# An interleave of two arrays in fp32: loads and stores spread over three DMA queues

## The chip, the cores and the metric

The kernel runs on one core of a Trainium2 chip. Times are device microseconds of one execution, and the figure compared is the median over several runs. The profile comes from one further execution, recorded by the hardware profiler; its own time and its span are given beside the median below.

Engines appear by short names: DVE is VectorE, ACT is ScalarE, POOL is GpSimd, SP is SyncE. A "q" behind the name (ACTq) means the engine's instruction queue, which issues DMAs. A DMA issued by any of them is carried out by the core's 16 DMA engines.

## The reference

Two arrays of 32 x 256 x 1024 fp32 (33.55 MB each) are interleaved element by element along the last axis:

```python
def reference(x, y):
    batch, seq, dim = x.shape               # 32, 256, 1024
    result = np.zeros((batch, seq, dim * 2), dtype=np.float32)
    result[..., 0::2] = x
    result[..., 1::2] = y
    return result
```

Nothing is computed; 67.1 MB are read and 67.1 MB written. Because the interleave pairs element k of x with element k of y, all three arrays can be treated as flat.

## The kernel before

**Tiles.** Each input is cut into 8 tiles of 128 partitions x 8192 fp32 (`WL`). A partition's row is 32 KB and contiguous in memory, so a tile is one contiguous 4.19 MB block and a load is 128 rows of 32 KB. Tile i of x and of y (`xtile`, `ytile`) are loaded at lines 56 and 57, both by SP. Each pool has two buffers, so the load of tile i+2 must wait until tile i has been copied.

**Copies and stores.** Every tile is worked off in two halves of 4096 columns (`WS`). For each half, line 70 copies x's half into the even columns of `otile`, and line 71 copies y's half into the odd columns, both on DVE. `otile` is 128 x 8192 fp32, so the store of one half (line 72, issued by ACT) is again 128 rows of 32 KB, 4.19 MB. `otile` has two buffers too: the copies of half n need the store of half n-2 to have landed. There are 16 loads, 32 copies and 16 stores.

**A first write.** Before the loop a small tile of zeros (16 x 128) is set by DVE (line 45) and written to the start of 16 output rows by ACT (line 47). The real stores write over it later.

**Order.** Every engine works through its own instructions in order, and semaphores order them among each other. SP's queue holds x0, y0, x1, y1 and so on; a y load is issued after the x load of its tile. ACT's queue holds the zero write and the stores. POOL has nothing in the loop.

**The opening.** After the program has been compiled, lines 86 to 104 take the first DMA that SP issues (x0, which waits for nothing) out of the body, and put it into the opening block ahead of SP's `Drain`, which belongs to the barrier of all engines at the start. So x0 is issued before that barrier, at 0.00 us of the span.

Of the kernel before, what the change touches and what calls it, by code (L numbers as in the profile page):

```python
# [2 lines left out]

# [4 lines left out]


@with_exitstack
def _interleave(
    ctx: ExitStack,
    tc: tile.TileContext,
    x: bass.AP,
    y: bass.AP,
    out: bass.AP,
):
    nc = tc.nc
    P = 128  # L20

    total = 1
    for s in x.shape:
        total *= s

    WL = 8192
    WS = 4096

    xf = x.rearrange("b s d -> (b s d)")
    yf = y.rearrange("b s d -> (b s d)")  # L30
    of = out.rearrange("b s d -> (b s d)")

    fp32 = mybir.dt.float32

    xpool = ctx.enter_context(tc.tile_pool(name="xp", bufs=2))
    ypool = ctx.enter_context(tc.tile_pool(name="yp", bufs=2))
    opool = ctx.enter_context(tc.tile_pool(name="op", bufs=2))

    lwidths = [WL] * (total // P // WL)
    assert sum(lwidths) == total // P  # L40


    wpool = ctx.enter_context(tc.tile_pool(name="wp", bufs=1))
    zero = wpool.tile([16, 128], fp32, name="zero")
    nc.vector.memset(zero, 0.0)  # L45
    first = dataclasses.replace(of, offset=0, ap=[[2 * WL, 16], [1, 128]])
    nc.scalar.dma_start(out=first, in_=zero)

    start = 0
    for lw in lwidths:  # L50
        xtile = xpool.tile([P, WL], fp32, name="xtile")[:, :lw]
        ytile = ypool.tile([P, WL], fp32, name="ytile")[:, :lw]

        xs = dataclasses.replace(xf, offset=start, ap=[[lw, P], [1, lw]])
        ys = dataclasses.replace(yf, offset=start, ap=[[lw, P], [1, lw]])
        nc.sync.dma_start(out=xtile, in_=xs)
        nc.sync.dma_start(out=ytile, in_=ys)

        soff = 0
        while soff < lw:  # L60
            width = min(WS, lw - soff)
            otile = opool.tile([P, 2 * WS], fp32, name="otile")[:, : 2 * width]
            os_ = dataclasses.replace(
                of,
                offset=2 * start + 2 * soff,
                ap=[[2 * lw, P], [1, 2 * width]],
            )
            xsub = xtile[:, soff : soff + width]
            ysub = ytile[:, soff : soff + width]
            nc.vector.tensor_copy(out=otile[:, 0::2], in_=xsub)  # L70
            nc.vector.tensor_copy(out=otile[:, 1::2], in_=ysub)  # L71
            nc.scalar.dma_start(out=os_, in_=otile)
            soff += width

        start += P * lw
    assert start == total


def kernel(tc, x, y, out):
    nc = tc.nc  # L80
    _interleave(tc, x, y, out)
    tc.close()
    tc.compile()  # L83


    blocks = nc.main_func.blocks
    opening = blocks[0].instructions
    at, moved = next(
        (b, i)
        for b in blocks[1:]  # L90
        for i in b.instructions
        if i.engine == mybir.EngineType.SP and i.opcode == "DMACopy"
    )
    assert not moved.sync_info.on_wait
    body = at.instructions
    body.remove(moved)
    gate = next(
        n
        for n, i in enumerate(opening)
        if i.engine == mybir.EngineType.SP and i.opcode == "Drain"  # L100
    )
    opening.insert(gate, moved)
    at.instructions = body
    blocks[0].instructions = opening


# [1 line left out]
_INS = ['x', 'y']  # L108
_OUTS = [((32, 256, 2048), 'float32')]


# [23 lines left out]
```

## Time and profile before

| | us |
|---|---|
| median of 4 runs | 315.93 (315.63 to 316.23) |
| the profiled execution's own time | 316.82 |
| its span (first to last instruction) | 315.0 |
| DVE busy | 72.8 |
| copies of line 70: 16, mean | 2.295 |
| copies of line 71: 16, mean | 2.292 |
| DVE idle before line 70, waiting for a store | 180.1 |
| DVE idle before line 71, waiting for y | 34.1 |
| x load, issue to landing (median) | 42.9 |
| y load, issue to landing (median) | 60.0 |
| store, issue to landing (median) | 29.9 |

The profile's page divides the span into 40 slices and gives for each the busy share of DVE and of the DMA engines in tenths, and the GB/s moved. "DMA out_dram<-otile" as the releaser of an idle stretch means that the engine waited for a store to land, which includes the time that the store stood in line. The mean over the span is 426 GB/s.

### The profile page before, as it was taken

How to read it: one execution, taken by the hardware profiler on the slowest of the kernel's cores; microseconds unless marked ns; L12 is line 12 of the kernel's file. 1: busy time of each engine (PE TensorE's matmuls, PEld its weight loads, DVE VectorE, ACT ScalarE, POOL GpSimd, SP SyncE). 2: the span in 40 equal slices, each digit the busy share in tenths (PEclk: the TensorE clock that was granted, in tenths of full speed). 3: DMA queues.
4: the chain of work that ended last, by engine and by line, in shares of the span. 5: the costliest groups of instructions: out<-in, count | busy, mean ns of one | idle time of the engine just before them, and what ended most of it. 6: DMA issues, size and time to landing. Idle time of an engine off the chain costs nothing.

```text
span 315.0 us, 152 instructions
## 1 busy us (share of the span) xinstructions
DVE 72.8 (23%) x33; POOL 0.2 (0%) x4
## 2 busy tenths in 40 slices
DVE  0334002213022220223203241041500405014500
POOL 0000000000000000000000000000000000000000
DMA  9999999999999999999999999999999999999996
GB/s 367 429 441 358 454 412 454 412 454 412 454 412 453 412 454 416 449 420 449 420 445 424 441 424 441 429 437 433 433 433 433 437 429 441 424 441 424 441 424 279
DMA packets 4641, 134.23 MB, mean 426 GB/s; under 512 B 529, under 2 KB 545, under 8 KB 545
## 3 DMA queue, kind: packets, MB, share of 16 engines
q1 hardware_dynamic: 2304, 67.11, 49.9%
q10 hardware_dynamic: 2336, 67.12, 49.3%
q14 instruction: 1, 0.00, 0.0%
HBM read 67.11 MB, written 67.12 MB: 426 GB/s over the span
## 4 chain that ended last, share of the span: by engine, by line
DMA 83%; DVE 11%; DVEq 1%; issue 0%
DMA out_dram<-otile 76%; DMA ytile<-in_y_dram 7%; DVE otile L71 6%; DVE otile L70 5%; DVEq L83 1%; DVEq L70 0%
## 5 line engine op out<-in xcount | busy, mean ns | idle before, releaser
L70 DVE COPY otile<-xtile 128x4096 f32<-128x4096 f32 x16 | 36.6, 2295 | 191.7 <-DMA out_dram<-otile 180.1
L71 DVE COPY otile<-ytile 128x4096 f32<-128x4096 f32 x16 | 36.6, 2292 | 34.1 <-DMA ytile<-in_y_dram 34.1
L45 DVE MEMSET zero<- 16x128 f32 x1 | 0.2, 165 | 0.9 <-PEq L119 0.9
L119 POOL MEMSET const-bfloat16-1.0<- 128x1 bf16 x1 | 0.1, 101 | 0.0
L119 POOL MEMSET const-uint8-127<- 128x1 uint8 x1 | 0.1, 101 | 0.0
L119 POOL MEMSET const-float32-0.0<- 128x1 f32 x1 | 0.1, 98 | 0.2 <-issue 0.2
L119 POOL MEMSET const-float32-1.0<- 128x1 f32 x1 | 0.1, 98 | 0.0
## 6 DMA issues: line engine op xcount, KB each, us to landing
out_dram<-otile ACTq DMA_DIRECT2D x16, 4096.0 KB, 29.9
xtile<-in_x_dram SPq DMA_DIRECT2D x8, 4096.0 KB, 42.9
ytile<-in_y_dram SPq DMA_DIRECT2D x8, 4096.0 KB, 60.0
out_dram<-zero ACTq DMA_DIRECT2D x1, 8.0 KB, 6.7
```

Source lines behind the costliest of these rows:

```text
L45: nc.vector.memset(zero, 0.0)
L70: nc.vector.tensor_copy(out=otile[:, 0::2], in_=xsub)
L71: nc.vector.tensor_copy(out=otile[:, 1::2], in_=ysub)
L83: tc.compile()
L119: nc = _bacc.Bacc("TRN2", target_bir_lowering=False, num_devices=1)
```

## The change

The stores and the zero write are issued by POOL (`nc.gpsimd`) instead of ACT, and the y loads by ACT instead of SP. The step that moves a DMA into the opening is run for SP and for ACT: x0 and y0 are then both issued ahead of the opening barrier, each by its own engine. Tiles, buffers and copies are the same.

```diff
-    nc.scalar.dma_start(out=first, in_=zero)
+    nc.gpsimd.dma_start(out=first, in_=zero)
...
         nc.sync.dma_start(out=xtile, in_=xs)
-        nc.sync.dma_start(out=ytile, in_=ys)
+        nc.scalar.dma_start(out=ytile, in_=ys)
...
-            nc.scalar.dma_start(out=os_, in_=otile)
+            nc.gpsimd.dma_start(out=os_, in_=otile)
...
-    opening = blocks[0].instructions
-    at, moved = next(
-        (b, i)
-        for b in blocks[1:]
-        for i in b.instructions
-        if i.engine == mybir.EngineType.SP and i.opcode == "DMACopy"
-    )
...
+    for engine in (mybir.EngineType.SP, mybir.EngineType.Activation):
+        opening = blocks[0].instructions
+        at, moved = next(
+            (b, i)
+            for b in blocks[1:]
+            for i in b.instructions
+            if i.engine == engine and i.opcode == "DMACopy"
+        )
+        assert not moved.sync_info.on_wait
+        body = at.instructions
+        body.remove(moved)
+        gate = next(
+            n
+            for n, i in enumerate(opening)
+            if i.engine == engine and i.opcode == "Drain"
+        )
+        opening.insert(gate, moved)
+        at.instructions = body
+        blocks[0].instructions = opening
```

More of the change, by code (lines that the diff above doesn't have):

```diff
@@ L86 @@
     blocks = nc.main_func.blocks
-    opening = blocks[0].instructions
-    at, moved = next(
-        (b, i)
-        for b in blocks[1:]
-        for i in b.instructions
-        if i.engine == mybir.EngineType.SP and i.opcode == "DMACopy"
-    )
[L94 to L104, printed above, removed]
+    for engine in (mybir.EngineType.SP, mybir.EngineType.Activation):
[17 more added lines that the diff above has]
+        blocks[0].instructions = opening
 _INS = ['x', 'y']
```

## The prediction

> **What bounds the kernel now.** I read the page first: the engines' busy time, the DMA row, the queue table and the chain.
>
> ```profile
> span 315.0 us, 152 instructions
> ...
> DVE 72.8 (23%) x33; POOL 0.2 (0%) x4
> ...
> DMA  9999999999999999999999999999999999999996
> ...
> q1 hardware_dynamic: 2304, 67.11, 49.9%
> q10 hardware_dynamic: 2336, 67.12, 49.3%
> ...
> DMA out_dram<-otile 76%; DMA ytile<-in_y_dram 7%; DVE otile L71 6%; DVE otile L70 5%; DVEq L83 1%; DVEq L70 0%
> ```
>
> VectorE works a quarter of the span. The 16 DMA engines are busy in every slice, and the two queues (q1 the loads, q10 the stores) fill 99.2% of their time. So VectorE's long waits for stores, and the 76% of the chain on `out_dram<-otile`, are waits for a transfer that stands in line behind others. The second view, stretches of the span with the GB/s in each, shows how much is left.
>
> ```profile
> 0.00:1.00 1.00, 0.14 (x1) 0.20 (x4) 1.00 0.00 0
> 1.00:2.00 1.00, 0.03 (x1) 0.00 (x0) 1.00 1.87 524
> 2.00:22.00 20.00, 4.50 (x2) 0.00 (x0) 1.00 0.97 420
> 22.00:34.00 12.00, 4.50 (x2) 0.00 (x0) 1.00 0.99 390
> 34.00:40.00 6.00, 0.00 (x0) 0.00 (x0) 1.00 1.01 437
> 40.00:312.00 272.00, 63.62 (x28) 0.00 (x0) 1.00 1.00 433
> 312.00:315.00 3.00, 0.00 (x0) 0.00 (x0) 1.00 0.08 33
> ```
>
> The last column is GB/s. From 40 to 312 us it is 433. The trace's records of single DMA packets agree: nearly every 32 KB packet took 1213 ns on its engine, load or store, alone or mixed (16 x 32768 B / 1.213 us = 432 GB/s). All bytes at 433 take 134.23 MB / 433 = 310.0 us, which leaves 5.0 of the 315.0:
> - about 1.0 us before the first byte and 0.4 us of ramp (0 to 22 us moved 8.92 MB, worth 20.6 us);
> - 1.2 us in 22 to 34 us, when the first real stores join: 12 x (433-390)/433. Load packets there took up to 2.9 us by the packet records;
> - the rest, some 2.4 us, at the end: engines that finish up to 1.5 us apart, the last landing, the closing barrier.
>
> The third view is the end, as a timeline, and SP's wait in it.
>
> ```profile
> 282.57 2.29 DVE L70 COPY otile<-xtile 128x4096 f32<-128x4096 f32 x1 [14.93 <-DMA out_dram<-otile]
> 288.87 2.30 DVE L71 COPY otile<-ytile 128x4096 f32<-128x4096 f32 x1 [4.00 <-DMA ytile<-in_y_dram]
> 291.20 8.65 ACTq L72 DMA_DIRECT2D out_dram<-otile  x2
> 294.98 2.29 DVE L70 COPY otile<-xtile 128x4096 f32<-128x4096 f32 x1 [3.81 <-DMA out_dram<-otile]
> 297.19 2.29 DVE L71 COPY otile<-ytile 128x4096 f32<-128x4096 f32 x1
> ```
> ```profile
> SPq L83 <- DMA out_dram<-otile: 19.3, 1, 19.3
> ```
>
> Number the stores 0 to 15. Store 13 lands at 294.9 and releases the last two copies; from there SP waits 19.3 us for stores 14 and 15, 8.39 MB, which is 434 GB/s. So the tail has no hole: store 15, issued at 299.5, was in line before store 14 landed at 294.9 + 9.7 = 304.6.
>
> **The change, part by part.** The bytes, their rate and the 16 engines stay. A cost counts only if it empties the engines or makes a packet slower.
>
> *Opening.* x0 is issued at 0.00 as before. y0 moves from 0.78 us on SP to about the same 0.0 on ACT. x0's packets alone kept the engines full to its landing at 12.6, so the earlier issue moves no byte sooner: gain 0, at most the 0.4 us ramp; at worst the two issues (0.37 us each) delay each other by one, 0.37. I take 0. x0 and y0 now share the engines, so x0 lands near 22 us instead of 12.6, and y0 at the 22.3 it had. The first L70 copies lose their head start (12.63): before, two L70 and one L71 were done by 24.65; now two or three copies of 2.2 to 2.3 us stand between 22.3 and store 0, so it goes out at 26.8 to 29 instead of 24.7, and x2 at about 29 instead of 17.15. Cover: x1 and y1, 8.39 MB = 19.4 us, fill the engines to 41.7. Cost 0.
>
> *y loads off SP.* On SP the y load stands behind x's, and its issue waited 13.5 us in all for L71. On ACT it waits for the same L71. Nothing is behind it there but the next y load. Cost 0. With two load rings against one of stores, I expect loads to take up to two thirds of the rate while both are queued, so y lands with x and the 34.1 us that L71 waits for y go to L70's wait for stores. Work is conserved: the stores get everything once the loads are in. The two buffers per pool still hold x(i+2) and y(i+2) back until the second half of tile i is copied.
>
> *17 stores onto POOL.* POOL has nothing to do after 0.43 us but the barriers, so nothing queues behind a store that waits for its L71, except the next store, which needs a later L71. The price is the time from L71's end to the first byte, which no row of before shows for this queue. From below: it equals ACT's issue, 0.34 us, and the 1.0 us that x0 took from issue to first byte, so 0 more. From above, by the tail: store 15 was issued 5.1 us before store 14 landed; less that 1.0 us, about 4 us are spare. A POOL issue up to 4 us longer costs nothing; beyond, each exposed store pays the excess. I take 0.
>
> *The rule that speaks against it.* The row: an L70 or L71 copy takes 2.29 us for 4096 fp32 per partition, 1.79 elements per ns, more than one per cycle at VectorE's 0.96 GHz. The Trainium skill (SBUF — State Buffer, section "SBUF: two separate sides") says of such two-port fp32 copies that GpSimd is locked out of its SBUF port while they run and cannot write descriptors for a DMA of its own queue; the DMA starts only when the copy ends. No row of before shows a DMA on that queue. Charged to every store at one copy, it is 16 x 2.3 = 37 us and 352. But the timeline shows what runs after an L71: VectorE sits idle, 14.9 or 10.6 us in the middle and 3.81 at the end, because the next copy needs the store before. Only store 0 has copies right behind it (2.2 to 4.5 us), under the 19.4 us of x1 and y1. By the rows the rule costs 0, also where it holds. Even a whole copy of delay, 2.3 us, is inside the 4 us.
>
> *First stores.* The 1.2 us of 22 to 34 us come again with the first store of another queue: gone (-1.2) or doubled (+1.2). The nearest row is the same event in before, so 1.2, change 0. The zero write stays as the queue's first use.
>
> *Packets.* If this queue's descriptors are also one per 32 KB row, 0. The packet records give a price for splitting: 27 ns for 512 B and 1213 for 32 KB make 8.2 ns fixed per packet, so n pieces per row add (n-1) x 8.2 ns x 128 store packets per engine = 1.05 us for each further piece. Fixed above by 4 KB pieces: 7 x 1.05 = 7.3 us. The row has only 32 KB packets; I take 0.
>
> *End.* The closing barrier (0.7 us after the last landing) already runs over POOL: 0, at most some tenths.
>
> **Sum.** 315.0 + 0 = 315.0 for the profiled execution's span. Its own time was 316.82, the median of the runs is 315.93; the runs without a profile are what is compared, so the forecast is 315.93 plus what the small unpriced terms, all on POOL's side (issue, completion), leave: 316.0. A measurement of this kernel can tell 0.2%, 0.6 us, from no change.
>
> **Rivals.**
> - *Faster.* The losses at the opening and the first stores shrink: ramp 0.4, first stores 1.2, and the engines' finish 1.5 us apart halves. For: they are the only non-433 stretches, and they lie where the change acts. Against: the same transfers start the same way. All of it is 0.4 + 1.2 + 0.8 = 2.4, half of it 1.2: 314.7.
> - *Slower by the store packets.* Each store row is cut into pieces on the software queue. It decides from two pieces on (1.05 us, above 0.6); at 4 KB pieces 323.2. For: another generator writes the descriptors. Against: no split in any row here.
> - *Slower by POOL's issue.* If descriptors take more than 4 us beyond ACT's issue, the tail opens: with two stores left that see it, 2 us of excess give 2 x 2 = 4 us, 319.9. Against: ACT's issue takes 0.34 us, a tenth of the slack.
> - *The change doesn't do what it says*, all DMAs being served as before: 315.9, inside the forecast.
>
> **How the numbers follow.** Forecast (316.0, own range 315.3 to 316.5): 0.40. Faster rival 0.26. Slower by packets 0.14, by POOL's issue 0.10, by several tenths from worse first stores or uneven engines 0.10. So faster 0.26, same 0.40, slower 0.34. Leaving out about 0.2, mostly the far end of splitting, the range is 314.7 to 320.0.
>
> **What would show it.** DMA 9 in every slice and 433 GB/s in the middle; three queues, with 67 MB stores on POOL's, 2048 store packets of data; L71's wait for y near 0, and L70's wait for stores up by about 30 us; first L70 near 22 us instead of 12.63; SP's last wait about 19.3 us for two stores. It is wrong if store packets are more than 2048, if GB/s in the store-only tail falls under 433, or if store landings at the end are more than 9.7 us apart: that would be POOL's issue.

## The result, and the profile after

The changed kernel has a median of 316.53 us (44 runs, 316.17 to 320.5) against 315.91 us for the kernel before (63 runs, 315.45 to 317.07). The ratio is 1.0045, with a 95% interval of 1.0033 to 1.0057: slower by about 1.4 us in the mean (the ratio compares means) and by 0.6 us in the median. The forecast was no change, 316.0.

The shape of the 44 times matters more than their median. 26 of them lie between 316.17 and 317.00, with a mean of 316.44; the other 18 lie between 317.16 and 320.5, with a mean of 318.88. Before's 63 runs have a mean of 316.01. So the mean moved by 1.43 us: 0.43 because even the usual run is longer, and 18/44 x (318.88 - 316.44) = 1.00 because of the second group. These are two effects, and the experiments look for the cause of each.

The lowest run rose by more than the usual one: 316.17 against 315.45, or 0.72 us. Before's runs spread over 1.6 us, the 26 usual runs over 0.8, so the usual run gets some of the 0.72 back.

The profiled execution took 316.38 us, a usual run. Before's profiled execution took 316.82, which is one of before's longer runs; what the two profiles show of the end must be compared with that in mind. First the page, in the parts that answer to those shown of before.

```profile
span 314.6 us, 150 instructions
...
DVE 72.0 (23%) x33; POOL 10.8 (3%) x21
...
q0 software_dynamic: 2336, 67.12, 49.4%
q1 hardware_dynamic: 1152, 33.55, 24.9%
q10 hardware_dynamic: 1152, 33.55, 24.9%
...
L71 DVE COPY otile<-xtile 128x4096 f32<-128x4096 f32 x16 | 36.7, 2294 | 225.3 <-DMA out_dram<-otile 143.5
L72 DVE COPY otile<-ytile 128x4096 f32<-128x4096 f32 x16 | 36.6, 2288 | 0.0
```

Three queues share the 16 engines. The stores' queue has 2336 packets, exactly what ACT's queue had: the software queue also makes one packet of each 32 KB row. The same two rows of before:

```profile
L70 DVE COPY otile<-xtile 128x4096 f32<-128x4096 f32 x16 | 36.6, 2295 | 191.7 <-DMA out_dram<-otile 180.1
L71 DVE COPY otile<-ytile 128x4096 f32<-128x4096 f32 x16 | 36.6, 2292 | 34.1 <-DMA ytile<-in_y_dram 34.1
```

The copies of y (now line 72) wait for nothing; their 34.1 us have gone into the wait of the x copies (225.3, against 191.7 + 34.1 = 225.8 before). Next the stretches, with GB/s in the last column.

```profile
1.00:2.00 1.00, 0.17 (x1) 0.52 (x1) 1.00 1.46 459
2.00:22.00 20.00, 0.24 (x1) 0.10 (x1) 1.00 0.97 420
22.00:34.00 12.00, 8.67 (x4) 2.54 (x2) 1.00 1.01 404
34.00:40.00 6.00, 0.00 (x0) 0.00 (x0) 1.00 0.99 426
40.00:312.00 272.00, 62.96 (x28) 7.44 (x14) 1.00 1.00 433
```

Little has moved here: the opening at 420; the dip at the first stores, a little later, with 0.1 MB more moved over the two stretches from 22 to 40 us; 433 in the long middle. By the trace's records of single packets the last packet ends at 312.77 us, where before's profile, of a long run, had 313.92, but the span ends only 0.4 us earlier. The time after the last packet is 1.83 us instead of 1.12, that is 0.71 more, and the lowest runs differ by 0.72. That is where the profile differs, and the next view shows why: the closing line's instructions in the queues of POOL and SP (durations in ns, least/median/most, then first and last start in us), first of before, then of after.

```profile
L83 POOLq EVENT_SEMAPHORE  x4: 17/17/17, 314.4 to 314.9; - x4
L83 POOLq DRAIN  x3: 34/41/70, 0.7 to 314.8; - x3
L83 SPq DRAIN  x3: 7/7/7, 314.3 to 314.6; - x3
```
```profile
L84 POOLq EVENT_SEMAPHORE  x4: 17/17/17, 313.9 to 314.5; - x4
L84 POOLq DRAIN  x3: 34/101/15236, 298.6 to 314.3; - x3
L84 SPq DRAIN  x3: 7/7/7, 313.2 to 314.1; - x3
```

SP has seen the last store land at 313.2 and is ready for the barrier. In before, POOL answers 0.1 us later (314.3, 314.4). In after, POOL has its own drain, issued with the last store at 298.6 and 15.24 us long: it ends at 313.85, 0.7 us after SP was ready, and only then does POOL answer (313.9).

### The profile page after: what moved, and what is told of

Same layout as the page of the kernel before. It is cut to its first block, busy times and chain, and to the rows that moved or that the text cites. A ratio compares the mean times of both kernels' runs of the same rounds, so it can differ in the third digit from the quotient of the medians.

```text
span 314.6 us, 150 instructions
## 1 busy us (share of the span) xinstructions
DVE 72.0 (23%) x33; POOL 10.8 (3%) x21
## 3 DMA queue, kind: packets, MB, share of 16 engines
q0 software_dynamic: 2336, 67.12, 49.4%
## 4 chain that ended last, share of the span: by engine, by line
issue 56%; DMA 31%; DVE 6%; POOL 2%; POOLq 0%; DVEq 0%
DMA out_dram<-otile 24%; DMA xtile<-in_x_dram 7%; DVE otile L71 3%; DVE otile L72 3%; POOL out_dram L73 2%; POOLq L84 0%; POOLq L73 0%; DVEq L71 0%
## 5 line engine op out<-in xcount | busy, mean ns | idle before, releaser
L71 DVE COPY otile<-xtile 128x4096 f32<-128x4096 f32 x16 | 36.7, 2294 | 225.3 <-DMA out_dram<-otile 143.5
L73 POOL DMA_DIRECT2D out_dram<-otile x16 | 10.0, 624 | 287.1 <-DVE otile L72 287.1
```

Source lines behind the costliest of these rows:

```text
L73: nc.gpsimd.dma_start(out=os_, in_=otile)
```

## The experiments

A ring is here the DMA queue of one issuing engine. The software queue is POOL's, which the profile calls `software_dynamic`. Three theories were to explain the two effects: POOL's drain (in every run), the software queue as such, or three rings in place of two. The changed kernel again, both loads on SP, y on POOL, and the last store on ACT were timed together on one chip; the others on other chips, all of them beside the kernel before.

**The changed kernel again.** No edit.

> The changed kernel unaltered, to see how its runs spread beside the others on one chip. Three theories of why its median is 0.6 us above before's and why 20 of 44 runs lie between 317 and 320.5: (drain) POOL's closing drain ends 0.7 us after the last store has landed, in every run; (software queue) stores through POOL's queue lose a further 1.5 to 4 us in some runs; (three rings) it is the two load rings beside the store ring, whatever generates the stores, that throw the 16 engines out of step in some runs. All three expect here a lowest run of 316.2 and about half the runs above 317; the median between 316.4 and 317.5. In the profile: last store landing about 0.7 us ahead of POOL's drain's end.

Measured 316.37 to 319.63, median 316.55; 2 of 12 runs above 317.5, fewer than expected. (The expectation says 20 of the first 44 lie above 317; by the list it is 18, and 17 lie above 317.5.) The profile shows the same end: POOL's drain ends 0.7 us after SP is ready. A third time:

> The changed kernel unaltered, on another occasion, since the kernels with the spare loads were not timed beside it: if the runs above 317 belong to the kernel, some 20 to 40% of them here (0 in 12 would have a chance of about 1 in 50 at 28%), lowest 316.2 to 316.4; if they belonged to one chip or one occasion, none.

316.31 to 319.4, 4 of 12 above 317.5, ratio 1.0046 (1.0025 to 1.0067). The longer runs belong to the kernel: 17, 2 and 4, that is 23 of 68 on three occasions. The share varies between them, from 2 of 12 to 17 of 44.

**Stores on POOL, both loads on SP**, run twice. Only x0 is issued in the opening, as in before.

```diff
-        nc.scalar.dma_start(out=ytile, in_=ys)
+        nc.sync.dma_start(out=ytile, in_=ys)
...
-    for engine in (mybir.EngineType.SP, mybir.EngineType.Activation):
+    for engine in (mybir.EngineType.SP,):
```

> Stores and zero write on POOL, both loads back on SP, only x0 in the opening: two rings. Drain: the lowest run stays 0.7 above before's, 316.2. Software queue: the long runs of 317 to 320 stay. Three rings: the long runs go, all runs within 316.2 to 317.1 (before's own spread of 1.6 plus the drain).

> Both loads on SP, stores on POOL, once more, for the count: if a single load ring keeps the engines together, all runs within 316.5 to 317.3 again; if the spread belongs to the software queue, some runs above 317.5.

316.64 to 317.19 (8 runs) and 316.59 to 317.09 (11 runs), ratio 1.0022 (1.0014 to 1.0031) in the second: no run above 317.5 in 19. All the stores are on the software queue, and the second group is gone. So the software queue of the stores is not enough to make it. (The first 8 ran beside the changed kernel, with its 2 of 12; the other 11 beside before and the kernels with spare loads below.) What remains is the closing; POOL's drain is again the longest (15.21 us from 298.9, so to 314.1, while SP was ready at 313.4). The lowest run lies 0.4 us above the changed kernel's, which was not expected. The packet records show where: the last packet ends at 313.04 and 313.17 instead of 312.77, and load packets in the first 50 us cost each engine 1.7 and 1.9 us on average instead of 1.35.

**y on POOL, stores on ACT**: three rings, another one in software. The zero write goes to ACT with the stores, and y0 stays in the body; these lines are left out below.

```diff
-        nc.scalar.dma_start(out=ytile, in_=ys)
+        nc.gpsimd.dma_start(out=ytile, in_=ys)
...
-            nc.gpsimd.dma_start(out=os_, in_=otile)
+            nc.scalar.dma_start(out=os_, in_=otile)
```

> Three rings, but y loads on POOL, stores and zero write on ACT; POOL's last DMA lands some 45 us before the end. Drain: the lowest run returns to before's 315.5. Software queue as a matter of stores: no long runs; as a matter of the queue itself: long runs as in the changed kernel. Three rings: long runs, 317 and above, stay in about half.

320.41 to 322.95 in all 5 runs, ratio 1.0183 (1.016 to 1.0205). The drain theory's expectation of 315.5 could not be read here, since this kernel is far slower for another reason. The packet records show it: packets, mostly of loads, that took up to 2.47 us instead of 1.213. They cost the engines 6.1 us each on average, 3.9 of it after 50 us, about 130, 170, 210 and 250 us. In before the same sum is 1.7 us, nearly all of it in the first 50 us. The engines had next to no idle gaps between packets. So the lost time is lengthened packets, not an empty queue.

**Both loads on POOL, stores on ACT**: two rings, loads in software. The zero write is on ACT too, and nothing is issued in the opening; these lines and that of the stores are left out below.

```diff
-        nc.sync.dma_start(out=xtile, in_=xs)
-        nc.scalar.dma_start(out=ytile, in_=ys)
+        nc.gpsimd.dma_start(out=xtile, in_=xs)
+        nc.gpsimd.dma_start(out=ytile, in_=ys)
```

> Both loads on POOL, stores and zero write on ACT, nothing in the opening: two rings, the software queue carries the loads. Three rings: no lengthened packets after 50 us and engines within 2.3 us of each other at the end, runs within about 1.5 us; time 316.5 to 317.7 (the first load leaves 1.3 us later than in before, plus 0.5 us of closing waits). Software queue slow for loads (rival for the 320.4 to 323.0 with y on POOL): 320 or more.

The profile (317.63, the lowest run) has no lengthened packet after 50 us and engines that end 0.32 us apart, as two rings should; the later opening costs it 1.6 us (first load packet at 2.6 instead of 1.0). But the six runs reach to 319.43, and the median of 318.02 is above the range expected. That spread isn't explained, and it keeps "two rings never spread" from being a rule.

**The last store on ACT**, the rest of the changed kernel as it is.

```diff
-            nc.gpsimd.dma_start(out=os_, in_=otile)
+            last = start + P * lw == total and soff + width == lw
+            (nc.scalar if last else nc.gpsimd).dma_start(out=os_, in_=otile)
```

> The changed kernel with only the very last store issued by ACT. Drain: if POOL's drain needs its own queue's last store, it ends some us before the last landing and the lowest run falls by 0.7 to 315.5; if the drain always takes its time after the end, 316.2 as before. Software queue and three rings: about half the runs still 1.5 to 4 us longer, as in the changed kernel.

316.21 to 318.75; 3 of 12 above 317.5. The lowest run fell by 0.16 only, from the 316.37 of the changed kernel beside it. The closing line again, of this kernel:

```profile
L85 SPq EVENT_SEMAPHORE  x10: 17/28/28, 315.7 to 316.9; - x10
...
L85 POOLq DRAIN  x3: 34/93/16432, 291.5 to 316.7; - x3
L85 SPq DRAIN  x3: 7/7/7, 316.2 to 316.5; - x3
```

POOL's long drain now runs from 291.5 for 16.43 us, so to 307.9, and holds nobody up: it ends 0.7 us after the landing of POOL's own last store (307.2), as the theory of the drain has it. Another wait took its place. SP waits at the close for the DMA semaphores two by two. The first wait was for the last store (landed 315.7; the time until then is not in the row, where no wait is longer than 28 ns). The seven waits left, for DMAs that were long done, took 62 ns each, until SP was ready at 316.2.

**The same, with SP's waits in the other order.** By the trace's semaphore records the DMAs from SP and ACT take turns on eight semaphores. Seven small loads that nothing uses move the last store to the semaphore that SP comes to last.

```diff
+        if start == P * lw:
+            few = dataclasses.replace(xf, offset=0, ap=[[WL, 16], [1, 128]])
+            for k in range(7):
+                spare = wpool.tile([16, 128], fp32, name=f"spare{k}")
+                nc.scalar.dma_start(out=spare, in_=few)
```

> Last store on ACT, and seven 8 KB loads into spare tiles on ACT after y1, so that the last store takes the semaphore that SP's closing waits come to last (they are extra work, nothing uses them). The run with the last store on ACT alone still ended 1.7 us after its last packet, because seven waits of 62 ns stood behind the last store's. Closing theory (POOL's drain, then SP's waits in series): the end now comes about 1.2 us after the last packet, and the lowest run is 315.6 to 315.8, against 316.2. If the floor of 316.2 has another cause: 316.2. Runs above 317 remain under the three-ring theory.

315.79 to 316.25 in 11 runs, ratio 1.0000 (0.9992 to 1.0009). Before's lowest run beside it was 315.59.

```profile
L91 SPq EVENT_SEMAPHORE  x10: 17/28/66212, 238.9 to 314.3; - x10
L91 POOLq EVENT_SEMAPHORE  x4: 17/17/17, 313.7 to 314.3; - x4
L91 POOLq DRAIN  x3: 34/101/16406, 289.3 to 314.1; - x3
L91 SPq DRAIN  x3: 7/7/7, 313.6 to 313.9; - x3
```

SP is ready at 313.6 and POOL answers at 313.7; from the last packet (313.17) to the end of the span are 1.2 us, as expected. That settles the first effect. The longer runs were gone as well, which was not expected, so this kernel ran once more, and the spare loads were tried alone.

> The kernel with the last store on ACT and seven spare loads, once more, since none of its 11 runs was above 316.3, where 28 of 75 runs of the three-ring kernels with x on SP and y on ACT were above 317. If that was chance: about a third of the runs above 317 here. If the spare loads or the moved store keep the engines together: none above 316.6, lowest 315.8 as before.

> The changed kernel, all stores on POOL, with the seven spare loads behind y1. Closing theory: lowest run 316.2 to 316.4, as in the changed kernel, since POOL's drain is last again. If the spare loads keep the engines together: no run above 317; if it was the last store on ACT, or chance: about a third above 317.

The kernel with the last store on ACT and the spare loads: 315.80 to 316.88, ratio 1.0002 (0.9992 to 1.0012). The changed kernel with the spare loads alone: 316.40 to 316.88 in 11 runs, ratio 1.0018 (1.0009 to 1.0027). Together with the earlier run, none of 33 is above 317.5. At a rate of one in three, or even at the 2 in 12 of the changed kernel's best occasion, that is hardly chance (about 1 in 400 at 2 in 12). The changed kernel itself was not timed beside them, but the kernel with y0 in the body (next) was timed beside the first of the three, and had 4 of 7. So it is the addition of the spare loads that removes the longer runs. With POOL on the last store again, 0.6 us of closing come back (316.40 against 315.80).

**y0 left in the body.**

```diff
-    for engine in (mybir.EngineType.SP, mybir.EngineType.Activation):
+    for engine in (mybir.EngineType.SP,):
```

> The changed kernel with y0 left in the body, so only x0 goes ahead of the opening barrier. Three rings: no matter, lowest run 316.2 to 316.4 and a third to a half of the runs above 317. If the two loads starting at the same instant throw the engines out of step: no runs above 317.2.

316.35 to 318.78, 4 of 7 above 317.5. The common start of x0 and y0 is not what makes the longer runs.

**x and y of a tile on one ring**, tiles in turn on SP and ACT.

```diff
-        nc.sync.dma_start(out=xtile, in_=xs)
-        nc.scalar.dma_start(out=ytile, in_=ys)
+        ring = nc.sync if start // (P * lw) % 2 == 0 else nc.scalar
+        ring.dma_start(out=xtile, in_=xs)
+        ring.dma_start(out=ytile, in_=ys)
```

> Three rings, but x and y of one tile share a ring: even tiles on SP, odd tiles on ACT; stores on POOL as in the changed kernel. If it takes two load rings active together beside the stores, few runs or none are above 317.4 here, since the loads of two tiles overlap little after the opening; if three rings in use are enough, a third to a half of the runs. Lowest run 316.2 to 316.7 (closing as in the changed kernel).

316.72 to 317.28, none of 6 above 317.5, ratio 1.0031 (1.0019 to 1.0043). That three rings in use are not enough, and that it takes x's and y's at once beside the stores, is a hint only: at one in three, 0 of 6 comes about by chance once in twelve times.

| kernel | rings: loads + stores | runs | lowest | above 317.5 |
|---|---|---|---|---|
| before, on all five occasions | x and y SP + ACT | 152 | 315.45 | 0 |
| changed, three times | x SP, y ACT + POOL | 68 | 316.17 | 23 |
| last store on ACT | the same | 12 | 316.21 | 3 |
| y0 in the body | the same | 7 | 316.35 | 4 |
| spare loads (three runs) | the same | 33 | 315.79 | 0 |
| x and y on SP (twice) | SP + POOL | 19 | 316.59 | 0 |
| tiles in turn | SP or ACT + POOL | 6 | 316.72 | 0 |
| y on POOL | x SP, y POOL + ACT | 5 | 320.41 | 5 |
| both loads on POOL | POOL + ACT | 6 | 317.63 | 6 |

In the last two rows the lowest run is already above 317.5, so the count says nothing of a second group there.

**What a longer run looks like.** The profile of the kernel with the last store on ACT fell on a run of 318.75. The timeline of its x copies stands beside that of the changed kernel's usual run: first the changed kernel, then the longer run.

```profile
174.02 2.29 DVE L71 COPY otile<-xtile 128x4096 f32<-128x4096 f32 x1 [11.20 <-issue]
...
251.47 2.29 DVE L71 COPY otile<-xtile 128x4096 f32<-128x4096 f32 x1 [11.21 <-issue]
...
274.49 2.30 DVE L71 COPY otile<-xtile 128x4096 f32<-128x4096 f32 x1 [18.52 <-DMA out_dram<-otile]
```
```profile
175.82 2.29 DVE L71 COPY otile<-xtile 128x4096 f32<-128x4096 f32 x1 [12.74 <-issue]
...
253.29 2.29 DVE L71 COPY otile<-xtile 128x4096 f32<-128x4096 f32 x1 [11.23 <-issue]
...
277.04 2.29 DVE L71 COPY otile<-xtile 128x4096 f32<-128x4096 f32 x1 [19.25 <-DMA out_dram<-otile]
```

The copies are 1.8 us late at 175 and 2.5 us late at 277, though the same bytes are moved. Each waits for a store to land on all engines. For two of the three the profile names no releaser (`<-issue`), but in the semaphore records a store lands about 0.1 us ahead of each: at 173.9 and 251.4 in the usual run, at 175.7 and 253.2 in the longer one. And the last stretches of that run, GB/s in the last column:

```profile
311.00:312.00 1.00, 0.00 (x0) 0.00 (x0) 1.00 1.21 524
312.00:313.00 1.00, 0.00 (x0) 0.00 (x0) 1.00 0.16 66
313.00:314.00 1.00, 0.00 (x0) 0.00 (x0) 1.00 0.00 0
314.00:315.00 1.00, 0.00 (x0) 0.00 (x0) 1.00 0.08 33
```

33 GB/s for 1 us is one packet of 32 KB: a single engine still works. The packet records do not name the engine of a packet; here a packet is put down to the engine whose last one had just ended, so the figures of single engines are estimates. By them 15 engines end between 312.6 and 313.5, and one at 315.3. That engine's load packets after 50 us were lengthened by 2.96 us in all, the others' by 0.3 to 0.9. In the changed kernel's usual run no engine lost more than 0.2 us there, and all ended within 0.5 us. The profile with y0 in the body (318.39) is a longer run as well: there the engines lost 0.8 to 2.5 us each to lengthened packets after 50 us, and all ended late, between 313.8 and 314.8. The losses come in bursts, within some 15 us after loads come back from a stretch in which the stores had the engines to themselves: of the profile with y0 in the body half falls between 160 and 180 us, of the one with the last store on ACT three quarters between 240 and 260. The bursts are not tied to stores: with y0 in the body 22 of the 27 us (summed over the engines) fall while at most four of the 16 engines carry a store, and load packets spend 72% of their time so in any case.

## Why the prediction was right and wrong

The median, 316.53, lies 0.5 us from the forecast and 0.03 above the forecast's own range. That it came so close is partly luck: more than half of the runs are usual ones, so the median leaves out the longer third, which the mean of 317.44 has. "No change" did not hold: the difference is small but clear of the noise. Term by term:

- *The bound* was right: 433 GB/s in the middle, before and after.
- *Opening and first stores* were right at 0: x0 landed at 21.7 us, and the first x copy began there.
- *y off SP* was right: y's wait went to the x copies' wait, and their sum stayed.
- *Packets* were right: one per 32 KB row, so the rival of split rows (0.14) falls. Stores land 9.7 us apart at the end (293.75, 303.45, 313.11), as forecast. One sign did not come: SP's last wait is 9.3 us, for store 15 alone, not 19.3 for two, because its waits stand in another order of semaphores.
- *POOL's issue and the rule on the shared port* were right in the sum. The rows of the stores in POOL's queue, of the changed kernel, with the copy beside the first one:

```profile
L73 POOL DMA_DIRECT2D out_dram<-otile x16: 531/531/2010, 26.6 to 298.6; - x16
```
```profile
26.17 2.29 DVE L71 COPY otile<-xtile 128x4096 f32<-128x4096 f32 x1
26.57 2.01 POOL L73 DMA_DIRECT2D out_dram<-otile  x1 [24.47 <-DVE otile L72]
```

  Fifteen stores took 0.53 us of POOL. Store 0 took 2.01, until 28.58, 0.12 us after the copy beside it ended at 28.46. This agrees with what the Trainium skill says (SBUF — State Buffer, section "SBUF: two separate sides"), that GpSimd cannot write its descriptors while such a copy runs, on the one store that the prediction named, and the loads in line covered it. The kernel with both loads on SP shows it again: 2.01 us from 24.53, so to 26.54, 0.11 us after the copies' end at 26.43. The slow-issue rival (0.10) falls too: POOL's 0.53 and some 0.3 us after the copy's end stay far under the 4 us that were spare.
- *End* is the first step that failed. The prediction took "0, at most some tenths" because the barrier already ran over POOL, and had no term for what POOL must itself wait for. It measured 0.7 us: POOL's own drain, which before took 0.07 us at most, now runs until 0.7 us after the last store of its queue has landed. The lowest runs show it, and moving both the last store and SP's order of waits took the lowest run to 315.79. The reading of before's end, "engines that finish up to 1.5 us apart", was of an execution 0.9 us above before's median.
- *Uneven engines* is the second. The prediction had "several tenths from worse first stores or uneven engines" at 0.10. The effect was partly named, but not its size (1 to 4 us) nor that it comes in a third of the runs, worth 1.0 us of the mean. The sentence that failed is "Work is conserved": in the two longer runs that were profiled the engines move every byte with hardly a gap and still lose time, because some packets, mostly of loads, take longer. What lengthens them stays open.

No version beat before. The best of the three-ring kernels, with the last store on ACT and the spare loads, equals it.

**What stays open.** What lengthens the packets isn't settled: the records show where and on which ring, not what the packet waited for. Why seven loads of 8 KB behind y1 prevent it isn't either. They do more than add bytes: y2 must wait for the first of them, whose semaphore it takes over (landed at 51.7), so it is issued at 51.7 us instead of 30.7 and lands at 98 instead of 76; and the later DMAs of SP and ACT get other semaphores. By 155 us x and y of a tile land within about 2 us of the changed kernel's again. Whether the later y2, the semaphores or the loads themselves matter was not tried; a kernel that only delays y2 would tell. Nor is it shown that three rings are the cause as such: tiles in turn use three as well, and had no longer run in 6. The spread of the kernel with both loads on POOL is open as well.

## What to carry to other kernels

Where the DMA engines are full, as here at 433 GB/s, another queue brought no bandwidth, and part of what it cost lay at the edge: look at the closing barrier of the engine that gets the queue, and give the last transfer to an engine whose drain is short. Look at the spread of the runs, not only at one profile: a profile of a usual run showed 0.4 us gained in the span while the mean lost 1.4, because it stood against one of before's longer runs (0.8 us above their mean) and was itself not one of the longer third (1.0 us of the mean). And when an ending is mended, look which wait is last next, since here seven waits of 62 ns took most of the gain.

## What was not expected of the hardware

POOL's drain after a store of its own queue ended 1.0 to 1.1 us after that queue's last packet, whether the store was the last of the program (312.77, 313.85) or not (306.85, 307.89); with y loads on POOL it was 0.7 us (279.81, 280.55). And the same three rings with another division of work (y through POOL, stores through ACT) were 4.4 to 7 us above the median of before, by packets of up to 2.47 us, while with two rings nearly every packet after the first 50 us took 1.213 us.
